# Dilated attention on one core: scores transposed, shifted by a fixed bound instead of row maxima, with the old form behind a flag

## The chip, the cores and the metric

One program runs on one core of one Trainium2 chip (the other seven cores are idle). The metric is the device time of one execution in microseconds (us), of which three runs before the change are known. Beside them stands one profiled execution, from which all durations below are read. The core has a matrix engine (PE, whose weight loads are listed as PEld), a vector engine (DVE), a scalar engine (ACT), a third elementwise engine (POOL) and a queue engine that only issues transfers (SP). Each runs its own list of instructions strictly in the order in which the program holds it, and waits on semaphores where an instruction needs another engine's result.

## The reference

One decoder layer on 2048 positions of 1024 columns: a norm and one input projection; two mixers beside each other, a short gated convolution and an attention of 8 heads of 64 columns; an output projection; a gated feed-forward part. The attention is what the change touches:

```python
q = rms_norm(q.reshape(B, S, N_HEADS, HEAD_DIM), g_q[l]) * (HEAD_DIM ** -0.5)
k = rms_norm(k.reshape(B, S, N_HEADS, HEAD_DIM), g_k[l])
...
for window, dil in ((128, 1), (512, 4), (2048, 16)):     # per head
    # query t attends to keys t, t-dil, ..., t-window
    s = where(valid, q k^T, -inf)
    m = max(s);  e = exp(s - m);  den = sum(e);  o = (e / den) v;  lse = m + log(den)
...
w = softmax(lses over the three branches);  o = sum(w * outs)
```

Since each branch is weighted by its own sum of exponentials, the result is one quotient: the three branches' sums of e·v over the three branches' sums of e, whatever number is subtracted from all scores of a row.

## The kernel before

All products are made in float16 pairs (a high and a low part, three matmuls per product), so a product of two float32 matrices costs three passes of PE.

The program's stages follow one another. First the input norm, the convolution's first three quarters and the weights' preparation. Then attention by four pairs of heads (`attention_pairs`, line 673; g = 0 to 3). Then the output projection (`out_b`) and the feed-forward part (`ffn`), which takes more than half of the span and isn't touched.

Within attention two generators run interleaved. `attn_steps(g)` (line 510) emits the attention of pair g; meanwhile `qkv_steps(g + 1)` (line 444) emits the projection of the next pair: 384 matmuls of 384 columns on PE (lines 188 to 190), then norm, split into high and low halves and three transposing transfers on the SP queue per 512 positions. For g = 3 the rest of the convolution and a first part of the output projection (`tail_steps`) take that place. How many projection steps stand beside one attention step is a number for each g (line 730). The final order on each engine is set by a scheduler ahead of the run.

Per head, `attn_steps` goes through three branches (b = 1, 2, 0: dilation 4, 16, 1), each of 16 tiles of 128 queries against one or two tiles of 128 keys. One step does this for two tiles with two key tiles each (14 steps a head) or for four tiles with one (5 steps a head):

- Scores (lines 612, 613): queries are the stationary operand, keys move, so a PSUM tile `s` has queries on its rows. The moving keys are high and low parts; a query row holds its own high and low part beside each other.
- Mask and row minimum of the negated scores in one DVE instruction per tile (line 618), each followed by a short read of the accumulator.
- Exponential with that row's own shift on ACT, one per tile (line 623).
- Split into float16 high and low: ACT copy (633), DVE subtraction (634).
- The values product needs keys on the rows, so the exponentials are transposed: in the 14 wide steps by a transposing transfer `et<-eh` of 128 x 1024 elements on the SP queue (line 635), in the 5 others by four PE transposes in float32 into PSUM `pt` (line 628).
- Values product (line 641): 128 x 65 columns into `av`, the 65th being the sum; an ACT copy brings it out (line 644).

`combine` (line 542) joins the three branches: their row shifts are compared, weights exp(difference) made, and POOL multiplies and adds 128 x 1040 tiles (lines 556 to 558), then divides (562). For the last head it runs on DVE in four pieces. Branches 1 and 2 go through memory (`d_u`, written in one order of rows and read back as `r` in another).

Queries lie in four-strided order (line 461 takes every fourth position as one tile), so a POOL copy `qn` (line 535) restores plain order for branch 0.

Of the kernel before, what the change touches and what calls it, by code (L numbers as in the profile page):

```python
# [18 lines left out]
P = 128  # L19
# [6 lines left out]
H = 8  # L26
# [4 lines left out]
class Builder:  # L31

# [163 lines left out]
    def run(self):  # L199
        tc, nc, A = self.tc, self.nc, self.A  # L200
        with ExitStack() as ctx:
# [5 lines left out]
            self.d_u = [[dr.tile([S, HD + 2], F32, name=f"d_u{h}_{b}") for b in range(2)] for h in range(H)]  # L207
# [10 lines left out]
            self.eps = cp.tile([P, 3], F32, name="eps")  # L218
            self.wsm = ctx.enter_context(tc.tile_pool(name="wsm", bufs=3))
            self.big = ctx.enter_context(tc.tile_pool(name="big", bufs=1))  # L220
            self.wq = ctx.enter_context(tc.tile_pool(name="wq", bufs=2))
            with ExitStack() as c1:
                e = c1.enter_context
                self.psmm = e(tc.tile_pool(name="psmm", bufs=3, space=PSUM))
                self.qk = e(tc.tile_pool(name="qk", bufs=2))
                self.mixer(c1)

                self.fs = ctx.enter_context(tc.tile_pool(name="fs", bufs=1, side="right"))
                self.fw = ctx.enter_context(tc.tile_pool(name="fw", bufs=15, side="right"))

                self.gs = ctx.enter_context(tc.tile_pool(name="gs", bufs=2, side="right"))
                self.psg = ctx.enter_context(tc.tile_pool(name="psg", bufs=4, space=PSUM, side="right"))
                self.out_b()
            self.ffn()

# [35 lines left out]
    def conv_steps(self, j, W, before=None, scratch=None):  # L271
# [12 lines left out]
        for c in range(S // NC):  # L284
# [49 lines left out]
            if j > 1:  # L334

                ps = self.pstr.tile([P, 4], F32, name="tr") if j < 3 else self.pst.tile([P, 4, P], F32, name="pt")[:, 0, 0:4]
# [107 lines left out]
    def qkv_steps(self, g, st):  # L444
# [8 lines left out]
        qT = self.qk.tile([P, 2, 4, 4, P], F16, name="qT")  # L453
        ka, kl = (self.qk.tile([P, 4, 2, 512], F16, name=nm, bufs=2) for nm in ("ka", "kb"))
        dv = self.d_v[g]
        for i in range(0, NT, 4):
            f = self.at.tile([P, 4, 4, HD], F32, name="qkf", bufs=2)
            for j in range(4):
                vs = self.vs[i // 4 % 2]

                t = slice(j, 4 * P, 4)
# [12 lines left out]
                if j == 3:  # L474
                    nc.sync.dma_start(dv[:, i * P:(i + 4) * P].rearrange("h (p t) c -> p h (t c)", t=4),
                                      vs.rearrange("p h t x d -> p h (t x d)"))
# [26 lines left out]
            for n_, dst in enumerate((qT.rearrange("p h j n t -> p (h j) n t")[:, :, i // 4],  # L503
                                      ka[:, i // 4].rearrange("p h (j t) -> p (h j) t", j=4),
                                      kl[:, i // 4].rearrange("p h (j t) -> p (h j) t", j=4))):
                self.transpose(dst, hl[:, 2 * n_:2 * n_ + 2].rearrange("p h j x d -> p (h j x d)"))
            yield
        st.update(qT=qT, ka=ka, kl=kl)

    def attn_steps(self, g, st):  # L510
# [4 lines left out]
        V, U, R = {}, {}, {}  # L515

        def load_v(h, b):
            dv = self.d_v[g][h]
            t = V[h, b] = self.vp.tile([P, NT, 2 * HD + 2], F16, name="v", bufs=2)
            if b == 1:  # L520
                nc.sync.dma_start(t.rearrange("p (n r) c -> p n (r c)", n=4),
                                  dv.rearrange("(n p r) c -> p n (r c)", n=4, r=4))
            elif b == 2:
                nc.sync.dma_start(t.rearrange("p r c -> p (r c)"), dv.rearrange("(p r) c -> p (r c)", r=16))
            else:

                for r in range(4):
                    nc.sync.dma_start(t[32 * r:32 * r + 32], dv.rearrange("(n p r) c -> r p n c", n=NT, r=4)[r])
        for h, b in [(h, b) for h in range(2) for b in (1, 2, 0)]:
            qT = st["qT"][:, h]  # L530
            ka, kl = (st[x][:, :, h] for x in ("ka", "kl"))
            if b == 1:
                qn = self.at.tile([P, S], F16, name="qn", bufs=1)
                for n in range(4):
                    nc.gpsimd.tensor_copy(qn[:, n * 512:(n + 1) * 512].rearrange("p (t j) -> p t j", j=4),
                                          qT[:, :, n].rearrange("p j t -> p t j"))
            load_v(h, b)


            last = g == 3 and h == 1  # L540

            def combine(c, n):
# [3 lines left out]
                w = self.at.tile([P, 3, NT], F32, name="cw", bufs=2)[:, :, 0:n]  # L546
                X = [r[:, ts] for r in (U[h, 0], R[h, 1], R[h, 2])]
                nc.vector.tensor_tensor(bm, X[0][:, :, HD + 1], X[1][:, :, HD + 1], op=ALU.min)
                nc.vector.tensor_tensor(bm, bm, X[2][:, :, HD + 1], op=ALU.min)
                for q in range(3):  # L550
                    nc.vector.tensor_tensor(w[:, q], bm, X[q][:, :, HD + 1], op=ALU.subtract)
                nc.scalar.activation(w, w, AF.Exp)
                X = [x[:, :, 0:HD + 1] for x in X]
                e = nc.vector if last else nc.gpsimd
                for q in range(3):
                    e.tensor_tensor(X[q], X[q], w[:, q].unsqueeze(2).broadcast_to([P, n, HD + 1]), op=ALU.mult)
                e.tensor_tensor(X[1], X[1], X[2], op=ALU.add)
                e.tensor_tensor(X[0], X[0], X[1], op=ALU.add)
                nc.vector.reciprocal(bm, X[0][:, :, HD])
# [6 lines left out]
            Ub = U[h, b] = self.up.tile([P, NT, HD + 2], F32, name="u", bufs=3)  # L566
            Vb = V[h, b]

            def query(u):

                if b == 0:
                    return qn[:, u * P:(u + 1) * P]
                if b == 1:
                    return qT[:, u % 4, u // 4]
                return qT[:, u % 4].rearrange("p n t -> p (n t)")[:, u // 4::4]

            def keys(tl, u, prev):

                k = tl.rearrange("p n (j t) -> p n j t", j=4)
                n = u // 4  # L580
                if b == 0:
                    m = u % 4
                    k = k.rearrange("p n j (m t) -> p n m j t", m=4)
                    if prev and m == 0:
                        return [k[:, n - 1, 3], k[:, n, 0]]
                    return [k[:, n, m - prev:m + 1]]
                if b == 1:
                    return [k[:, n - prev:n + 1, u % 4]]
                return [k[:, :, u % 4, u // 4::4]]

            mask = self.masks[b == 0]

            def has_prev(u):
                return 1 if (b == 0 and u > 0) or (b == 1 and u >= 4) else 0
            for u0 in (0, 8, 4, 12) if last and b == 0 else range(0, NT, 4):
                av = self.psav.tile([P, 4, HD + 1], F32, name="av")

                four = not has_prev(u0 + 3)
                for us in (range(u0, u0 + 4),) if four else (range(u0, u0 + 2), range(u0 + 2, u0 + 4)):


                    blocks = [(u, x) for u in us for x in range(1 - has_prev(u), 2)]
                    nb = len(blocks)
                    at = {u: slice(P * blocks.index((u, 1 - has_prev(u))), P * blocks.index((u, 1)) + P) for u in us}
                    sp = self.pss.tile([P, 512], F32, name="s")
                    for u in us:
                        pv = has_prev(u)
                        hi, lo = keys(ka, u, pv), keys(kl, u, pv)
                        w = (at[u].stop - at[u].start) // len(hi)
                        for x in range(len(hi)):  # L610
                            o = sp[:, at[u].start + x * w:at[u].start + (x + 1) * w]
# [620 lines left out]
```

## Time and profile before

| | us |
|---|---|
| three runs | 2168.03, 2169.90, 2171.61 (median 2169.90) |
| the profiled execution, whole | 2167.63 |
| its span, first to last instruction | 2165.8 |

| stage in the profiled execution | from, to (us) |
|---|---|
| input norm, convolution, weights, projection of pair 0 | 0 to 295 |
| attention of the four pairs, with the next pair's projection beside it | 295 to 752 |
| last head's end and start of the output projection | 752 to 800 |
| output projection | 800 to 930 |
| feed-forward part | 930 to 2166 |

The stages' limits are read from the first and the last matmul of each kind: the first score matmul starts at 285 us and the last at 751 us, and the last values product at 776 us. PE is busy for 2062.4 us of the span (95%), DVE for 1412.4, ACT for 1031.5 and POOL for 657.8. A matmul's row shows from its issue to its modelled end, so rows of PE overlap and a busy PE can still have room: how closely matmuls start behind one another says more than their duration.

### The profile page before, as it was taken

How to read it: one execution, taken by the hardware profiler on the slowest of the kernel's cores; microseconds unless marked ns; L12 is line 12 of the kernel's file. 1: busy time of each engine (PE TensorE's matmuls, PEld its weight loads, DVE VectorE, ACT ScalarE, POOL GpSimd, SP SyncE). 2: the span in 40 equal slices, each digit the busy share in tenths (PEclk: the TensorE clock that was granted, in tenths of full speed). 3: DMA queues.
4: the chain of work that ended last, by engine and by line, in shares of the span. 5: the costliest groups of instructions: out<-in, count | busy, mean ns of one | idle time of the engine just before them, and what ended most of it. 6: DMA issues, size and time to landing. Idle time of an engine off the chain costs nothing. (4 is left out here: it accounts for less than half of the span.)

```text
span 2165.8 us, 32715 instructions
## 1 busy us (share of the span) xinstructions
PE 2062.4 (95%) x11864; PEld 1071.6 (49%) x11864; DVE 1412.4 (65%) x3206; ACT 1031.5 (48%) x2166; POOL 657.8 (30%) x547
## 2 busy tenths in 40 slices
PE   4899999999898889999999999999999999999999
PEld 2344577777665534444444444444444444444444
DVE  6687437677666866885766666666676665545454
ACT  6443347777765745662433333333333344343341
POOL 0001134454532311310312111211121145555463
PEclk9999999999999989999999999999999999999999
DMA  9867459999989977899332233223322763241442
GB/s 248 170 199 240 125 128 161 209 187 205 192 165 225 207 181 237 231 296 228 102 117 83 93 103 112 88 88 107 112 89 88 253 250 86 88 165 54 128 139 93
DMA packets 555491, 339.63 MB, mean 157 GB/s; under 512 B 354624, under 2 KB 508224, under 8 KB 552896
## 3 DMA queue, kind: packets, MB, share of 16 engines
q1 hardware_dynamic: 537648, 314.38, 56.3%
q10 hardware_dynamic: 17680, 23.16, 3.0%
q8 instruction: 93, 1.52, 0.3%
q14 instruction: 70, 0.57, 0.1%
HBM read 161.24 MB, written 107.54 MB: 124 GB/s over the span
## 5 line engine op out<-in xcount | busy, mean ns | idle before, releaser
L1012 PEld LDWEIGHTS <-w 128*128 128x128 f16 x3696 | 363.0, 98 | 454.4 <-issue 21.7
L1012 PE MATMUL ps<-b,w 128*128 128x512 f16 x2112 | 468.7, 383 | 12.0 <-DMA b<-d_h 4.8
L1143 PE MATMUL ps<-b,w 128*128 128x512 f16 x1848 | 399.8, 379 | 3.8 <-DVE s L1164 2.3
L1012 PE MATMUL ps<-hb,w 128*128 128x512 f16 x1584 | 347.1, 379 | 0.0
L1143 PEld LDWEIGHTS <-w 128*128 128x128 f16 x1848 | 180.8, 98 | 222.6 <-issue 5.2
L905 POOL TENSOR_TENSOR t<-wq 128x512 f32<-128x512 f32 (+1 forms) x46 | 60.0, 1304 | 410.4 <-issue 236.8
L1018 DVE TENSOR_TENSOR s<-ps,s 128x512 f32<-128x512 f32 x220 | 150.0, 683 | 37.0 <-PE ps L1012 36.5
L188 PE MATMUL mm<-wq,b 128*128 128x384 f16 x512 | 167.7, 327 | 0.0
L189 PE MATMUL mm<-wq,b 128*128 128x384 f16 x512 | 167.5, 327 | 0.0
L190 PE MATMUL mm<-wq,b 128*128 128x384 f16 x512 | 167.4, 327 | 0.0
L1150 POOL TENSOR_TENSOR x<-x,s 128x512 f32<-128x512 f32 x72 | 103.6, 1440 | 173.1 <-DVE s L1164 134.1
L1151 DVE SCALAR_TENSOR_TENSOR x<-ps,a_u,x 128x512 f32<-128x512 f32 x96 | 71.8, 749 | 101.4 <-PE ps L1143 74.8
L618 DVE CUSTOM_DVE_ANT_0 s<-s,mask,nkap 128x256 f32<-128x256 f32 (+1 forms) x224 | 104.4, 483 | 41.4 <-PE s L613 37.1
L623 ACT ACTIVATE s<-s,u 128x256 f32<-128x256 f32 (+1 forms) x224 | 100.0, 457 | 37.4 <-DVE u L618 31.6
L922 ACT CAST w<-t 128x512 f16<-128x512 f32 x88 | 53.7, 616 | 132.6 <-PE ps L1012 66.3
L188 PEld LDWEIGHTS <-b 128*128 128x128 f16 x768 | 83.8, 109 | 62.0 <-ACT b L786 8.4
L189 PEld LDWEIGHTS <-b 128*128 128x128 f16 x768 | 83.9, 109 | 56.2 <-issue 6.8
L190 PEld LDWEIGHTS <-b 128*128 128x128 f16 x768 | 83.7, 109 | 54.9 <-issue 2.6
L188 PE MATMUL cvx<-b,wq 128*128 128x512 f16 (+1 forms) x200 | 77.3, 390 | 31.2 <-ACT kb L265 24.9
L641 PE MATMUL av<-v,et 128*128 128x65 f16 x1800 | 77.5, 195 | 29.9 <-DMA et<-eh 22.1
L634 DVE TENSOR_TENSOR eh<-s,eh 128x512 f16<-128x512 f32 (+1 forms) x112 | 75.6, 678 | 35.4 <-ACT eh L633 35.1
L1121 ACT ACTIVATE wq<-wq,asf 128x512 f32<-128x512 f32 x88 | 56.6, 710 | 86.6 <-DMA wq<-d_a 86.6
(302 smaller groups left out, 3783.1 us busy)
## 6 DMA issues: line engine op xcount, KB each, us to landing
d_a<-a ACTq DMA_DIRECT2D x88, 256.0 KB, 2.0
d_wd<-w SPq DMA_DIRECT2D x77, 256.0 KB, 2.0
wq<-d_a SPq DMA_DIRECT2D x64, 256.0 KB, 4.1
b<-d_wd SPq DMA_DIRECT2D x14, 1024.0 KB, 6.4
wraw<-in_w_in_dram SPq DMA_DIRECT2D x24, 512.0 KB, 7.2
d_h<-hl SPq DMA_DIRECT2D x24, 512.0 KB, 3.2
wq<-in_w_gate_dram SPq DMA_DIRECT2D x22, 512.0 KB, 5.2
wq<-in_w_up_dram SPq DMA_DIRECT2D x22, 512.0 KB, 5.4
```

What stands on the lines that cost most here:

```text
L188: self.pe = mm(ps, lhsT=lh(k), rhs=rh(k), start=k == ks[0], stop=False)
L189: mm(ps, lhsT=lh(k), rhs=rl(k), start=False, stop=False)
L190: mm(ps, lhsT=ll(k), rhs=rh(k), start=False, stop=k == ks[-1])
L618: nc.vector.tensor_tensor_reduce(sm[:, at[u]], sp[:, at[u]], mask[:, P - P * has_prev(u):256], accum_out=Ub[:, u, HD + 1:HD + 2], op0=ALU.add,
L623: nc.scalar.activation(sm[:, at[u]], sm[:, at[u]], AF.Exp, scale=-1.0, bias=Ub[:, u, HD + 1:HD + 2])
L634: nc.vector.tensor_tensor(eh[:, w:2 * w], sm[:, 0:w], eh[:, 0:w], op=ALU.subtract)
L641: self.pe_av = nc.tensor.matmul(av[:, u - u0], lhsT=p_, rhs=v_, start=n_ == 0, stop=n_ == len(ops) - 1)
L1012: nc.tensor.matmul(ps[self.BANK[n]], lhsT=w[:, x, k], rhs=b[:, y, k], start=first and k == 0 and q == 0, stop=k == 3 and q == 2, skip_grou ...
L1018: nc.vector.tensor_tensor(t, x, y, op=ALU.add)
L1143: nc.tensor.matmul(ps[self.BANK[n]], lhsT=L[n][:, x, f], rhs=B[n][:, f, y], start=first and f == 0 and q == 0, stop=f == n_f - 1 and q == ...
L1150: nc.gpsimd.tensor_tensor(o, o, s_, op=ALU.add)
L1151: nc.vector.scalar_tensor_tensor(o, bank, u, o, op0=ALU.mult, op1=ALU.add)
```

## The change

The scores are made transposed (keys stationary, queries moving), so that the exponentials come out with keys on the rows, as the values product needs them. No transpose of any kind is left between them. Row maxima can't be had cheaply in this form, so all scores are shifted by one number: both operands are normalised, so no score is above 8 times the largest product of gains (`bound`). The branches then need no weights; `combine` adds three sums and divides.

```diff
-  for u in us:   # each tile of 128 queries: hi, lo = its one or two tiles of keys
-      nc.tensor.matmul(o, lhsT=query(u), rhs=hi[x], start=True, stop=False)
-      nc.tensor.matmul(o, lhsT=query(u), rhs=lo[x], start=False, stop=True)
-      nc.vector.tensor_tensor_reduce(sm[:, at[u]], sp[:, at[u]], mask[...], accum_out=Ub[:, u, HD + 1:HD + 2], ...)
-      nc.scalar.activation(sm[:, at[u]], sm[:, at[u]], AF.Exp, scale=-1.0, bias=Ub[:, u, HD + 1:HD + 2])
-  if four:
-      nc.tensor.transpose(pt[:, x], sm[:, x * P:(x + 1) * P], self.ident32)
...
-  else:
...
-      self.transpose(et, eh)
+  runs = [(u, u, 1) for u in pr]            # b == 2: four tiles
+  runs = [(u, u, 2), (w, w, 1)]             # b < 2: two tiles, and (u - step, u, 1) ahead where there are such keys
+  for kb_, u, n in runs:                    # a tile of keys against n tiles of queries
+      for i, k in enumerate(keys(kb_)):
+          nc.tensor.matmul(sp[:, o:o + n * P], lhsT=k, rhs=queries(u, n), start=i == 0, stop=i == 1)
+  if b < 2:
+      nc.vector.tensor_tensor(sp[:, 0:o], sp[:, 0:o], self.masks[b][:, 512 - o:512], op=ALU.add)
+  nc.scalar.activation(dst, src, AF.Exp, scale=self.kap, bias=self.bound)
+  if b == 2:
+      nc.gpsimd.affine_select(e, e, pattern=[[0, 4], [1, P]], compare_op=ALU.is_ge, fill=0.0, ...)
+  nc.scalar.copy(et[:, 0], e)
+  nc.vector.tensor_tensor(et[:, 1], e, et[:, 0], op=ALU.subtract)
```

A head has 20 steps in place of 19. Positions now stay in plain order: the projection's stationary operand is contiguous (`slice(j * P, (j + 1) * P)`), and the keys of branch 1 and 2 are read as a strided stationary operand, every 4th and every 16th column. The queries of these branches come from a copy `q16` that POOL regroups (32 copies of 512 columns in place of the 32 of `qn`):

```diff
+  o, d = ((u * P, 1), (u // 4 * 512 + u % 4, 4), (u, 16))[b]
+  return [k[:, o:o + (P - 1) * d + 1:d] for k in (ka, kl)]
...
+  self.nc.gpsimd.tensor_copy(st["q16"][h][:, :, 32 * n:32 * n + 32], st["qT"][:, n, h].rearrange("p (a r) -> p r a", r=NT))
...
-  for n_, dst in enumerate((qT..., ka..., kl...)):      # three transposing transfers of 128 x 1024
-      self.transpose(dst, hl[...])
+  self.transpose(qT[:, i // 4]..., hl[:, 0:2]...)       # one of 128 x 1024
+  for h in range(2):
+      for n_, dst in ((2, ka), (4, kl)):                # four of 128 x 512
+          self.transpose(dst[:, h, i * P:(i + 4) * P]..., hl[:, n_ + h]...)
```

`combine` loses its weights and keeps the least sum for a check:

```diff
-  nc.vector.tensor_tensor(bm, X[0][:, :, HD + 1], X[1][:, :, HD + 1], op=ALU.min)
...
-  nc.scalar.activation(w, w, AF.Exp)
-  for q in range(3):
-      e.tensor_tensor(X[q], X[q], w[:, q].unsqueeze(2).broadcast_to([P, n, HD + 1]), op=ALU.mult)
   e.tensor_tensor(X[1], X[1], X[2], op=ALU.add)
   e.tensor_tensor(X[0], X[0], X[1], op=ALU.add)
+  nc.vector.tensor_reduce(self.dmin[:, d:d + 1], X[0][:, :, HD], axis=AX.X, op=ALU.min)
+  nc.vector.tensor_scalar_max(bm, X[0][:, :, HD], 2.0 ** -7)
```

The values `d_v` are written in plain order, two transfers of 130 columns a row in place of one of 520, the rows of `d_u` are 65 columns in place of 66, PSUM has two `av` tiles in place of one and no `pt`, and the steps of projection beside one step of attention are 4.29, 3.32, 3.04 and 2.0 in place of 4.52, 3.49, 3.2 and 2.1.

A fixed shift can make all of a row's exponentials tiny. So the whole old kernel stands behind the new one, as a second program (`General`) that runs if a sum was below 2^-6:

```diff
+  def check(self):
+      nc.vector.tensor_single_scalar(self.dmin, self.dmin, 2.0 ** -6, op=ALU.is_lt)
+      nc.vector.tensor_copy(self.low, self.vmax(self.dmin))
+  def otherwise(self):
+      rv = self.nc.values_load(self.low[0:1].bitcast(I32), min_val=0, max_val=0x3F800000, ...)
+      with self.tc.If(rv > 0):
+          General(self.tc, self.A).run()
```

On the inputs of the reference the least sum, worked out from its own formulas, is 2.9 and the threshold is 0.016, so the flag is 0.

How the order moves. On PE, in the attention of the last pair before the change: `s` are scores, `pt` the float32 transposes, `av` the values product, L188 to L190 the convolution.

```order
L613 LDWEIGHTS qT
L613 MATMUL s<-kb,qT 128x128
L628 MATMUL pt<-ident_99,sm 128x128 x2
L612 LDWEIGHTS qT
L612 MATMUL s<-ka,qT 128x128
L628 MATMUL pt<-ident_99,sm 128x128
L641 LDWEIGHTS et
L641 MATMUL av<-v,et 128x65
```

The same pair after the change, in branch 0: a full step is now six score matmuls, of which four stand here, with the keys `ka`, `kb` as stationary operand.

```order
L627 LDWEIGHTS ka
L627 MATMUL s<-qT,ka 128x256
L627 LDWEIGHTS kb
L627 MATMUL s<-qT,kb 128x256
L627 LDWEIGHTS ka
L627 MATMUL s<-qT,ka 128x128
L627 LDWEIGHTS kb
L627 MATMUL s<-qT,kb 128x128
```

No `pt` row is left, and operands have changed sides. On the SP queue before the change, in the attention of pair 0's second head: `d_u` and `r` are a branch's results on their way through memory, `d_v` and `v` the values, `qkhl` the next pair's queries and keys.

```order
L655 DMA r_4031<-d_u_0_67 128x16x66
L475 DMA d_v_62<-vs_2121 128x2x520
L196 DMA_TRANSPOSE et<-eh 128x6x128
L196 DMA_TRANSPOSE et<-eh 128x8x128 x2
L196 DMA_TRANSPOSE qT<-qkhl 128x8x128
L196 DMA_TRANSPOSE ka<-qkhl 128x8x128
L196 DMA_TRANSPOSE kb<-qkhl 128x8x128
L196 DMA_TRANSPOSE et<-eh 128x8x128
L653 DMA d_u_1_68<-u 128x1056
```

The queue after the change, at the same place:

```order
L667 DMA r_3978<-d_u_0_67 128x16x65
L497 DMA d_v_62<-vs_2132 128x4x130 x2
L198 DMA_TRANSPOSE qT<-qkhl 128x8x128
L198 DMA_TRANSPOSE ka<-qkhl 128x4x128
L198 DMA_TRANSPOSE kb<-qkhl 128x4x128
L198 DMA_TRANSPOSE ka<-qkhl 128x4x128
L198 DMA_TRANSPOSE kb<-qkhl 128x4x128
L665 DMA d_u_1_68<-u 128x1040
```

All `et<-eh` rows are gone, and nothing that PE's values product waits for is queued there but `v`. At the end of the same queue after the change:

```order
L1202 DMA out_dram<-x_15_17552 128x1024
L1202 DMA out_dram<-x_7_17544 128x512
L251 TENSOR_LOAD low
L253 COMPARE_AND_BRANCH
L280 DMA nx_x<-in_x_dram 128x1024 x2
```

Before the change the list ended with the second of these transfers. Now each engine loads the flag and branches over the second program, whose first row is the last one shown.

More of the change, by code (lines that the diff above doesn't have):

```diff
@@ L31 @@
 class Builder:
+    W = HD + 1
     def __init__(self, tc, A):
@@ L206, in run @@
             self.d_v = [dr.tile([2, S, 2 * HD + 2], F16, name=f"d_v{g}") for g in range(4)]
-            self.d_u = [[dr.tile([S, HD + 2], F32, name=f"d_u{h}_{b}") for b in range(2)] for h in range(H)]
+            self.d_u = [[dr.tile([S, self.W], F32, name=f"d_u{h}_{b}") for b in range(2)] for h in range(H)]
             self.d_wq = [dr.tile([P, 2, KC, 384], F16, name=f"d_wq{g}") for g in range(5)]
@@ L218, in run @@
             self.eps = cp.tile([P, 3], F32, name="eps")
+            self.dmin = cp.tile([P, 11], F32, name="dmin")
+            self.low = cp.tile([P, 1], F32, name="low")
             self.wsm = ctx.enter_context(tc.tile_pool(name="wsm", bufs=3))
@@ L452, in qkv_steps @@
         yield
-        qT = self.qk.tile([P, 2, 4, 4, P], F16, name="qT")
-        ka, kl = (self.qk.tile([P, 4, 2, 512], F16, name=nm, bufs=2) for nm in ("ka", "kb"))
+        qT = self.qk.tile([P, 4, 2, 512], F16, name="qT")
+        ka, kl = (self.qk.tile([P, 2, S], F16, name=nm, bufs=2) for nm in ("ka", "kb"))
+        st.update(qT=qT, ka=ka, kl=kl, q16=[self.at.tile([P, NT, P], F16, name="q16", bufs=2), None])
         dv = self.d_v[g]
@@ L577, in keys @@
[L577 to L589, printed above, removed]
@@ new lines, in queries, with keys @@
+                    return q16.rearrange("p (x j) (n a) -> p j n x a", j=4, n=4)[:, u % 4, u // 4:u // 4 + n]
+                return q16[:, u]
+            def keys(u):
+                o, d = ((u * P, 1), (u // 4 * 512 + u % 4, 4), (u, 16))[b]
+                return [k[:, o:o + (P - 1) * d + 1:d] for k in (ka, kl)]
+            step = 4 if b == 1 else 1
+            if b == 1:
+                tiles = [[4 * n + j for j in (j0, j0 + 1) for n in (n0, n0 + 1)] for n0 in (0, 2) for j0 in (0, 2)]
+            else:
+                tiles = [list(range(u0, u0 + 4)) for u0 in ((0, 8, 4, 12) if last and b == 0 else range(0, NT, 4))]
@@ L657, in attn_steps, with pools, few, constants @@
                 combine(0, NT)
+    def pools(self, e):
+        tc = self.tc
+        self.pss = e(tc.tile_pool(name="pss", bufs=3, space=PSUM))
+        self.psav = e(tc.tile_pool(name="psav", bufs=2, space=PSUM))
+    def few(self):
+        return self.pss.tile([P, 512], F32, name="s")[:, 0:4]
+    def constants(self, m, u):
+        nc = self.nc
+        self.masks = []
+        for b in range(2):
+            mask = self.at.tile([P, 512], F32, name=f"mask{b}")
+            nc.gpsimd.memset(mask, 0.0)
+            for x in range(4):
+                sg = 1 if x % 2 else -1
+                t = mask[:, x * P:(x + 1) * P].rearrange("p (x a) -> p x a", x=4)
+                pattern = [[32 * sg, 4], [sg, 32]] if b == 0 else [[sg, 4], [4 * sg, 32]]
+                nc.gpsimd.affine_select(t, t, pattern=pattern, compare_op=ALU.is_ge, fill=-1e30, base=0,
+                                        channel_multiplier=-sg)
+            self.masks.append(mask)
+        self.kap = self.at.tile([P, 1], F32, name="kap")
+        nc.vector.tensor_scalar_mul(self.kap, u, HD ** -0.5 * 2.0 ** -22)
+        self.bound = self.at.tile([P, 1], F32, name="bound")
+        nc.vector.tensor_scalar(self.bound, m, -HD ** 0.5, 15 * math.log(2.0), op0=ALU.mult, op1=ALU.add)
+    RATES = (4.29, 3.32, 3.04, 2.0)
     def attention(self):
```

395 lines of the change are left out of this document (299 added, 96 removed).

## The prediction

> **What bounds the kernel now.** I read the page first, from the top.
>
> ```profile
> span 2165.8 us, 32715 instructions
> ...
> PE   4899999999898889999999999999999999999999
> ...
> PEclk9999999999999989999999999999999999999999
> DMA  9867459999989977899332233223322763241442
> ```
>
> One slice is 54 us. PE is full nearly everywhere; attention (slices 6 to 14) is where it shows gaps, and where the transfer engines are full too. The table of stretches puts numbers on that stage, and beside it the output projection as a dense one.
>
> ```profile
> core 0: us, PE busy (x) PEld busy (x) DVE busy (x) ACT busy (x) POOL busy (x), PEclk, DMA share, GB/s
> 295.00:752.00 457.00, 427.49 (x4242) 318.27 (x4240) 307.90 (x1115) 328.81 (x885) 196.47 (x157) 0.98 0.96 192
> 752.00:800.00 48.00, 37.42 (x197) 16.77 (x198) 33.79 (x124) 20.77 (x52) 7.31 (x12) 0.81 0.83 193
> 800.00:930.00 130.00, 127.11 (x582) 57.18 (x581) 96.90 (x180) 79.17 (x140) 29.60 (x24) 0.99 0.78 232
> ```
>
> In the 457 us of attention PE is busy for 427, and the 16 transfer engines for 96%. DVE (67%), ACT (72%) and POOL (43%) have room. In the 48 us behind it PE loses 10.6 us idle, and its clock is granted at 0.81. Attention is thus bound by PE, with stalls. The table of waits names them, for 295 to 752 us and, in the last row, for 752 to 800:
>
> ```profile
> PEld L641 <- DMA et<-eh: 28.2, 23, 4.5
> PE av L641 <- DMA et<-eh: 20.9, 19, 4.2
> ...
> PE mm L188 <- ACT b L786: 7.8, 2, 6.5
> ```
>
> The first two rows are the same stalls, seen at the weight load and at the matmul: the values product waits for a transposing transfer. I count the larger, 28.2 us, once. How densely PE works between stalls is read from starts in the timeline of PE:
>
> ```profile
> 432.04 0.89 PE L641 MATMUL av<-v,et 128*128 128x65 f16 x24
> 432.77 0.27 PE L612 MATMUL s<-ka,qT 128*128 128x256 f16 x1
> 432.88 0.27 PE L613 MATMUL s<-kb,qT 128*128 128x256 f16 x1
> ...
> 433.76 0.33 PE L188 MATMUL mm<-wq,b 128*128 128x384 f16 x1
> 433.93 0.33 PE L189 MATMUL mm<-wq,b 128*128 128x384 f16 x1
> ...
> 437.89 0.30 PE L612 MATMUL s<-ka,qT 128*128 128x128 f16 x1
> 438.00 0.30 PE L613 MATMUL s<-kb,qT 128*128 128x128 f16 x1
> 438.12 0.30 PE L612 MATMUL s<-ka,qT 128*128 128x128 f16 x1
> ...
> 442.54 0.63 PE L628 MATMUL pt<-ident,sm 128*128 128x128 f32 x4
> 443.01 0.28 PE L613 MATMUL s<-kb,qT 128*128 128x128 f16 x1
> ```
>
> From start to start a score matmul of 256 columns takes 0.11 us, one of the projection (384) 0.17, a values product 0.73/24 = 0.030, and a float32 transpose 0.47/4 = 0.117. The scores of branch 2 (437.89 to 438.12) take 0.117 for 128 columns, twice the 0.055 that half of the 256 row would make: both operands are read there with every fourth element.
>
> **The change part by part.** The sum is made against the profiled execution, 2167.6 us (span 2165.8), which lies 2.3 us under the median of the three runs.
>
> *PE transposes go.* All 160 of them:
>
> ```profile
> L628 PE MATMUL pt<-ident,sm 128*128 128x128 f32 x160 | 28.1, 279 | 0.0
> ```
>
> 160 x 0.117 = 18.7 us of PE's own time on the bounding engine: **-19**.
>
> *Transposing transfers go.* 112 of them, 3.8 us each from issue to landing, and up to four in a row on the queue:
>
> ```profile
> et<-eh SPq DMA_TRANSPOSE x112, 3.8
> ...
> 431.63 3.71 SPq L196 DMA_TRANSPOSE et<-eh  x2
> 436.07 8.40 SPq L196 DMA_TRANSPOSE et<-eh  x4
> ```
>
> The values product then waits for DVE's subtraction directly, so the 28.2 us go: **-28**. The queue keeps `v`, `d_u`, `r`, `d_v` and five transposes per 512 positions where it had three, of the same bytes; with 112 issues fewer ahead of them they come earlier, and of PE's waits in attention none of any size names them now. I cost them at nothing; the cover is that they are prefetched a step or a branch ahead.
>
> *Elementwise work.* For these groups in attention:
>
> ```profile
> L618 DVE CUSTOM_DVE_ANT_0 s<-s,mask,nkap 128x256 f32<-128x256 f32 x215 | 101.5, 488 | 36.6 <-PE s L613 35.1
> L623 ACT ACTIVATE s<-s,u 128x256 f32<-128x256 f32 x214 | 96.4, 461 | 29.7 <-DVE u L618 23.9 <-DVE qkr_t L486 2.5 <-DVE qkr_t L485 0.9
> L634 DVE TENSOR_TENSOR eh<-s,eh 128x512 f16<-128x512 f32 x102 | 69.8, 688 | 32.1 <-ACT eh L633 31.9
> L633 ACT CAST eh<-s 128x512 f16<-128x512 f32 x103 | 61.4, 601 | 15.9 <-DMA et<-eh 14.8
> L623 ACT ACTIVATE sm<-sm,u 128x128 f32<-128x128 f32 x156 | 52.8, 405 | 8.7 <-DVE u L618 8.4
> L618 DVE CUSTOM_DVE_ANT_0 sm<-s,mask,nkap 128x128 f32<-128x128 f32 x156 | 45.4, 346 | 31.9 <-PE pt L628 16.0 <-PE s L613 14.6 <-ACT et L629 1.2
> L618 DVE DVE_READ_ACCUMULATOR2_ANT u<- 128x1 f32 x378 | 44.3, 117 | 0.0
> ...
> L1154 ACT ACTIVATE s<-ps,a_u 128x512 f32<-128x512 f32 x24 | 16.4, 682 | 17.6 <-issue 12.5 <-PE ps L1143 5.1
> ```
>
> DVE loses 101.5 + 45.4 + 44.3 = 191 us and gains 128 masks at about 0.69 (the 634 row), 88: 308 becomes some 205. ACT loses 96 + 53 = 149 and gains 160 exponentials at 0.68 (the 1154 row), 109: 329 becomes some 290. POOL loses the weights of seven heads (21 tiles) and gains 32 selections of 512 columns:
>
> ```profile
> L685 POOL TENSOR_SCALAR_AFFINE_SELECT mask<-mask x4: 292/300/313, 249.4 to 250.2; 128x128 f32<-128x128 f32 x4
> ...
> L556 POOL TENSOR_TENSOR r<-r,cw 128x1040 f32<-128x1040 f32 x14 | 26.7, 1929 | 35.0 <-ACT cw L552 35.0
> ```
>
> 21 x 1.93 = 41 us go, 32 x 4 x 0.30 = 38 come; the copies `q16` take the place of as many `qn`. None of the three becomes the bound of a stage of about 457 - 19 - 28 = 410 us, all of it beside PE. What does lie on a path is new: branch 2 now goes through POOL, and behind a selection wait ACT's copy, DVE's subtraction and PE's values product. POOL is in order, and ahead of a selection can stand a 1.9 us tile or a copy that waits for a transfer. Nothing in the trace prices that wait: at the low end it is nothing (PE has the projection to do), at the high end 32 selections each behind one 1.9 us tile, 61 us. The nearest case is DVE's group of 634, whose waits for ACT cost PE almost nothing; I take **+5**, for eight blocks of four.
>
> *The scores.* Columns are the same; 128 more matmuls are only longer ones cut in two, which costs nothing at 0.055 per 128. What is unknown is a strided stationary operand under short matmuls. If the moving side made the 0.117, branch 2's 256 matmuls fall to 0.055: -16. If the stationary side made it, branch 2 stays, and branch 1's 192 short ones rise by 0.062: +12, its 128 long ones by 0.007: +1. If the wider step of 16 doubles branch 2's, 256 x 0.117 = 30 more: +43. The projection's rows have a stationary operand strided by four before the change and start every 0.17 us for 384 columns, no slower than the 256 rows for their size. So I leave branch 1 as its size makes it and branch 2 at its own old row: **0**, with -16 and +43 as ends.
>
> [...]
>
> *End of attention.* From 752 to 800 us PE loses 10.6 us idle and 0.19 x 37.4 = 7 us of clock, 17.7 in all, part of it to the last transposes and the last head's `combine`, which loses its weights; 7.8 us are a wait for ACT that the change leaves. I take half: **-9** (0 to -18). In attention the clock is 0.98, worth 9 us, a third of which should return with the stalls: **-3** (0 to -9).
>
> *The flag.* Each engine loads a register and jumps. On SP this stands behind the last transfer's issue:
>
> ```profile
> L1179 SPq DMA_DIRECT2D out_dram<-x x17: 332/333/351, 2069.5 to 2162.9; - x17
> ...
> DMA to landing us min/median/max: 2.0/2.6/3.8
> ```
>
> It is hidden if it takes less than the landing (2.0), and costs up to two round trips (7.6) if it isn't: **+2**. If the branch were taken, the whole old program would run behind, some 2166 us; the least sum of 2.9 against 0.016 excludes it.
>
> Sum: -19 - 28 + 5 + 0 - 9 - 3 + 2 = -52, so 2167.6 - 52 = **2116 us**.
>
> **The rivals.**
>
> *Strided keys are slow.* Price +13 to +43, so 2129 to 2159 us. For it: branch 2's row at twice its size. Against it: the projection's strided operand. By the Trainium skill ("SBUF — State Buffer", on its 16-byte lines) reads that touch a line only once pay, which speaks for this rival in branch 2, whose step of 16 float16 is 32 bytes; but by the same rule the old step of 8 bytes should have been free, and the 0.117 differs from that.
>
> *PE fills up.* Moving operands were the slow side (-16), the other half of the end (-9) and the rest of the clock (-6) return, and nothing new waits (-5): 2080 us. For it: the dense stretch 800:930 shows what PE does when fed.
>
> *Slower: the chain between scores and values product.* PE's order is fixed ahead. A step's mask, exponential, copy and subtraction take 0.69 + 0.68 + 0.60 + 0.69 = 2.7 us, and PE's share of a step is about 410/160 = 2.6. If the order leaves only one step between, or ACT's other work (70% busy) holds up the exponential, PE waits in every step. It decides from 0.33 us per step (160 x 0.33 = 52); at 0.5 us the time is 2168 + 28 = 2196 us. For it: PE's waits for the old chain. Against it: that chain was longer by 3.8 us of transfer, and the new order keeps two or three steps between a score and its product in the pieces I read.
>
> **How the numbers follow.** Forecast 0.58 (its own range 2100 to 2132), strided keys 0.18, PE filled 0.15, slower 0.08, anything with the second program 0.01. The range 2085 to 2150 leaves out the slow cases (0.09) and the far halves of the two others. A measurement tells 0.2% (4 us) from no change: faster 0.89, same 0.02, slower 0.09.
>
> **What would show it.** In the profile after: no wait of PE for `et`; about 455 us between the first score and the end that now takes 505; DVE and ACT below 75% there; starts of branch 2's scores 0.055, 0.117 or 0.23 us apart; PE's waits for the subtraction or the selection under 10 us; the span's end 2 to 5 us behind the last store's issue. Wrong would make it: PE waiting in most steps for ACT or DVE, or a jump at the end that takes over 10 us.

## The result and the profile after

| | before, us | after, us |
|---|---|---|
| median | 2168.97 (2167.75 to 2171.61, 4 runs) | 2134.12 (2127.46 to 2136.36, 4 runs) |
| the profiled execution, whole / span | 2167.63 / 2165.8 | 2136.36 / 2134.9 |
| first score matmul | 285.0 | 300.9 |
| last values product | 776.3 | 729.3 |
| first matmul of the feed-forward part | 941.1 | 908.2 |

The ratio is 0.9833 with a 95% interval of 0.9809 to 0.9857: 34.8 us faster by the medians, 31.3 by the two profiled executions. The forecast was 52. The feed-forward part starts 32.9 us earlier, so the whole gain lies ahead of it. I use the stretch from 285 us to the first matmul of the feed-forward part as the stage to compare, since work of the projection and the convolution moves freely within it: the first score starts 15.9 us later because PE takes up the next pair's projection first, and is busy for all of that time. The page of the kernel after, its span and busy tenths:

```profile
span 2134.9 us, 31526 instructions
...
PE   4899999989899899989999999999999999999998
...
PEclk9999999999999899999999999999999999999999
DMA  9866445656575757896233223322332772331442
```

In attention the transfer engines have fallen from mostly 9 tenths to 5 to 7, but PE's row has hardly filled: four 8s there have become three. The table of stretches for this stage, first of the kernel before:

```profile
285.00:941.00 656.00, 613.01 (x5137) 404.31 (x5136) 451.68 (x1444) 439.55 (x1097) 236.33 (x194) 0.97 0.91 200
```

and of the kernel after (columns as in the prediction: length, then PE, PEld, DVE, ACT, POOL busy, PE's clock, DMA share):

```profile
285.00:908.00 623.00, 582.78 (x5108) 360.45 (x5106) 416.21 (x776) 435.42 (x870) 232.47 (x204) 0.97 0.63 163
```

PE is busy 30.2 us less, but idle for 40.2 us where it was 43.0. The change took work off PE and hardly any waiting. The waits of PE's weight loads in the kernel after, from 280 to 800 us, show who took the place of the transfers:

```profile
PEld L649 <- DVE et L644: 27.1, 25, 3.7
PEld L649 <- ACT et L643: 7.9, 14, 1.2
```

29.6 us of waiting for `et<-eh` by the same window (28.2 from 295 to 752 us) have become 27.1 for the subtraction and 7.9 for the copy ahead of it. The groups of instructions show that these cost more than was forecast:

```profile
L644 DVE TENSOR_TENSOR et<-sm,et 128x512 f16<-128x512 f32 (+1 forms) x160 | 148.0, 940 | 70.9 <-ACT et L643 70.0
L638 ACT ACTIVATE sm<-s,bound,kap 128x512 f32<-128x512 f32 (+1 forms) x160 | 146.6, 940 | 45.1 <-DVE s L632 43.0
L643 ACT CAST et<-sm 128x512 f16<-128x512 f32 (+1 forms) x160 | 94.4, 612 | 4.7 <-POOL sm L640 3.0 <-PE av L649 0.8
L632 DVE TENSOR_TENSOR s<-s,mask 128x512 f32<-128x512 f32 (+1 forms) x128 | 80.6, 650 | 26.9 <-PE s L627 26.4
L640 POOL TENSOR_SCALAR_AFFINE_SELECT sm<-sm 128x512 f32<-128x512 f32 x32 | 23.9, 749 | 51.9 <-ACT sm L638 28.5 <-DVE qT L336 19.0 <-DVE et L644 4.3
```

Masks (650 ns) and copies (612) cost what was said. The subtraction takes 940 ns in place of 690 and the exponential 940 in place of 680. The view of the single line shows that the subtraction's mean is not its usual length (minimum, median, maximum):

```profile
L644 DVE TENSOR_TENSOR et<-sm,et x160: 496/693/2757, 304.3 to 728.1; 128x512 f16<-128x512 f32 x120, 128x384 f16<-128x384 f32 x40
```

The median is the forecast's 690, but 39 of 160 take over 1.0 us and 15 over 2.0. The old form's subtraction, with its input in PSUM, never did:

```profile
L634 DVE TENSOR_TENSOR eh<-s,eh x112: 549/687/693, 305.7 to 756.7; 128x512 f16<-128x512 f32 x104, 128x384 f16<-128x384 f32 x8
```

What stands beside the long ones is seen in the timeline, here all engines ahead of PE's longest wait for one:

```profile
679.91 0.56 DVE L644 TENSOR_TENSOR et<-sm,et 128x384 f16<-128x384 f32 x1 [0.54 <-ACT et L643]
...
680.42 2.41 POOL L580 TENSOR_TENSOR r<-r,r 128x1040 f32<-128x1040 f32 x1 [18.59 <-DMA r<-d_u]
680.52 2.85 DVE L335 SCALAR_TENSOR_TENSOR qT<-ka,convw,qT 128x512 f32<-128x512 f32 x1
...
682.91 2.70 POOL L581 TENSOR_TENSOR u<-u,r 128x1040 f32<-128x1040 f32 x1
683.30 2.72 DVE L644 TENSOR_TENSOR et<-sm,et 128x384 f16<-128x384 f32 x1
...
686.08 0.57 PE L649 MATMUL av<-v,et 128*128 128x65 f16 x7 [3.61 <-DVE et L644]
```

Two DVE instructions that take 0.75 and 0.55 us elsewhere each end 0.4 to 0.5 us behind the POOL tile beside them (682.83 and 685.61), and PE waits 3.61 us for the second. Worked out from all 160 subtractions: the 94 with POOL idle beside them take 0.694 us at most, those that start ahead of POOL's instruction keep their usual length (as at 679.91), and each of the 39 over 1.0 us ends a fixed time behind the end of a POOL instruction, 0.41 to 0.42 us at 384 columns and 0.54 to 0.56 at 512, however long it took. That is a hold until POOL's instruction ends and not a sharing of pace. The sum's tiles end only 11 of these 39; the others stand behind the next pair's norm, splits and query copies (lines 510 to 540) and, once, a selection. The masks on the same engine, with one operand in PSUM, do not move (682 to 700 ns at 512 columns).

The Trainium skill ("SBUF — State Buffer", section "SBUF: two separate sides") says that DVE and GpSimd (POOL here) share one port pair of SBUF, that a DVE instruction with two SBUF inputs beside a GpSimd instruction that reads SBUF, or a DVE instruction in a mode that uses both ports, takes it alone, and that whoever comes second waits for the other's whole instruction. The rows agree: 2.85 and 2.72 us beside tiles of 2.41 and 2.70. In the old form the subtraction's input `s` lay in PSUM; after the change it is `sm` in SBUF.

### The profile page after: what moved, and what is told of

Read it like the earlier page. It is cut to its first block, busy times and chain, and to the rows that moved or that the text cites. A ratio compares the mean times of both kernels' runs of the same rounds, so it can differ in the third digit from the quotient of the medians.

```text
span 2134.9 us, 31526 instructions
## 1 busy us (share of the span) xinstructions
PE 2029.4 (95%) x11832; PEld 1021.3 (48%) x11832; DVE 1378.0 (65%) x2538; ACT 1027.4 (48%) x1939; POOL 655.4 (31%) x562
## 5 line engine op out<-in xcount | busy, mean ns | idle before, releaser
L644 DVE TENSOR_TENSOR et<-sm,et 128x512 f16<-128x512 f32 (+1 forms) x160 | 148.0, 940 | 70.9 <-ACT et L643 70.0
L190 PE MATMUL mm<-wq,b 128*128 128x384 f16 x512 | 168.7, 330 | 1.8 <-DVE vs L494 1.8
L638 ACT ACTIVATE sm<-s,bound,kap 128x512 f32<-128x512 f32 (+1 forms) x160 | 146.6, 940 | 45.1 <-DVE s L632 43.0
L649 PE MATMUL av<-v,et 128*128 128x65 f16 x1800 | 90.2, 195 | 28.2 <-DVE et L644 22.3
L190 PE MATMUL cvx<-b,wq 128*128 128x512 f16 (+1 forms) x200 | 77.3, 390 | 31.8 <-DMA b<-ka 24.5
L191 PEld LDWEIGHTS <-b 128*128 128x128 f16 x768 | 75.9, 99 | 63.1 <-issue 9.2
L190 PEld LDWEIGHTS <-b 128*128 128x128 f16 x768 | 75.8, 99 | 62.0 <-ACT b L809 5.0
L192 PEld LDWEIGHTS <-b 128*128 128x128 f16 x768 | 75.7, 99 | 60.9 <-issue 2.7
L649 PEld LDWEIGHTS <-et 128*128 128x128 f16 x1800 | 78.3, 99 | 48.3 <-DVE et L644 27.1
L1067 ACT ACTIVATE sg<-s,w_un 128x512 f32<-128x512 f32 x66 | 47.3, 719 | 106.1 <-DVE s L1041 98.2
```

What stands on the lines that cost most here:

```text
L190: self.pe = mm(ps, lhsT=lh(k), rhs=rh(k), start=k == ks[0], stop=False)
L191: mm(ps, lhsT=lh(k), rhs=rl(k), start=False, stop=False)
L192: mm(ps, lhsT=ll(k), rhs=rh(k), start=False, stop=k == ks[-1])
L638: nc.scalar.activation(dst, src, AF.Exp, scale=self.kap, bias=self.bound)
L644: nc.vector.tensor_tensor(et[:, 1], e, et[:, 0], op=ALU.subtract)
L649: self.pe_av = nc.tensor.matmul(av[:, us.index(u)], lhsT=p_, rhs=v_, start=n_ == 0, stop=n_ == len(ops) - 1)
```

## The experiments

Theory 1: the subtraction is held up by POOL, and PE with it. Theory 2: branch 1's exponential, which writes every fourth element, loads ACT. Theory 3: neither; PE's fixed order puts the values product too close behind its scores, whatever the durations. Theory 4: branch 2's way through POOL. All runs had five rounds beside the kernel before, whose medians lie between 2167.2 and 2168.9 us. "Idle" is the stage's length less PE's busy time in it, from the table of stretches; "waits" are PEld's waits for the subtraction and for the copy. Stage, idle, mean and waits are read from one execution each, whose own time lies up to 6 us from the median.

| run | median, us | ratio (95% interval) | stage | idle | L644 mean, ns | waits |
|---|---|---|---|---|---|---|
| changed, again | 2131.2 | 0.9830 (0.9814 to 0.9846) | 618 | 37.9 | 936 | 24.1 + 9.3 |
| no flag | 2127.3 | 0.9818 (0.9799 to 0.9836) | 616 | 37.5 | 931 | 24.3 + 9.9 |
| sum left out | 2108.0 | 0.9718 (0.9703 to 0.9734) | 594 | 22.8 | 802 | 11.7 + 6.1 |
| plain exponential | 2118.8 | 0.9774 (0.9756 to 0.9791) | 611 | 32.8 | 909 | 21.4 + 4.5 |
| stride on the read | 2120.6 | 0.9787 (0.9774 to 0.9801) | 611 | 31.0 | 895 | 18.0 + 5.0 |
| branch 0 in PSUM | 2123.4 | 0.9799 (0.9782 to 0.9816) | 612 | 33.4 | 877 / 670 | 13.7 + 12.7 |
| branches 0, 1 in PSUM, plain | 2098.4 | 0.9675 (0.9660 to 0.9691) | 586 | 17.8 | 844 / 645 | 6.8 + 5.3 |
| all in PSUM | 2095.1 | 0.9663 (0.9647 to 0.9679) | 585 | 14.1 | 653 | 6.9 + 4.4 |
| sum on DVE | 2126.3 | 0.9805 (0.9788 to 0.9821) | 618 | 37.0 | 789 | 26.3 + 7.2 |
| sum in quarters | 2120.9 | 0.9784 (0.9762 to 0.9805) | 613 | 34.4 | 816 | 23.4 + 7.4 |
| 21 more POOL tiles | 2148.8 | 0.9909 (0.9889 to 0.9930) | 638 | 56.1 | 915 | 37.1 + 9.8 |
| all in PSUM, 21 more tiles | 2109.3 | 0.9725 (0.9705 to 0.9744) | 603 | 26.6 | 652 | 7.5 + 13.2 |

(Two means: subtractions that read SBUF / PSUM.)

**The changed kernel again.** 

> The changed kernel as it is, beside the others on one chip: 2128 to 2136 us; its PE waits for L644 between 22 and 28 us. It says how far one profile of it strays.

Measured 2131.2; the profiled execution is 10 us shorter than the first, its idle time 2.3 us and its waits for the subtraction 3.0 us less, with the same order on every engine. Differences of that size between two profiles say nothing. Differences below are against this run.

**No flag.** Leaves out the jump and the second program.

```diff
-        self.otherwise()
```

> Leaves out the register load and jump at the end and the second program behind it. If the jump is not hidden by the last store: 3 us less (the last matmul to the end of the span 4.1 us as before the change, against 7.2). If it is hidden: no difference, and 7.2 us stay.

DVE's last row and the issue of the last stores, of the changed kernel (span 2134.9):

```profile
2126.80 2.46 SPq L1202 DMA_DIRECT2D out_dram<-x  x2
2128.15 0.75 DVE L1174 SCALAR_TENSOR_TENSOR x<-ps,a_u,x 128x512 f32<-128x512 f32 x1 [1.38 <-PE ps L1166]
```

and DVE's last row without the flag (span 2124.2):

```profile
2120.46 0.75 DVE L1173 SCALAR_TENSOR_TENSOR x<-ps,a_u,x 128x512 f32<-128x512 f32 x1 [1.38 <-PE ps L1165]
```

From DVE's last instruction to the end it is 6.0 us with the flag and 3.0 without: 3.0 us, not hidden. The kernel before has 3.0 too. The medians differ by 3.9, within their intervals.

**The sum left out.** For seven heads POOL neither adds the branches nor divides.

```diff
-  e.tensor_tensor(X[1], X[1], X[2], op=ALU.add)
-  e.tensor_tensor(X[0], X[0], X[1], op=ALU.add)
+  if last: ...                       # the division likewise
```

The number kept for the flag is the greatest sum here and not the least.

> Leaves out the sum over the three branches and its scaling for seven of the eight heads (21 tiles on POOL, 49.5 us in the changed kernel); nothing is put in its place. Theory 1 (the subtraction L644, whose two inputs now both lie in SBUF, is held up while POOL works): the mean of L644 falls from 940 to about 850 ns, PE's waits for it from 27 to about 15 us, time 6 to 12 us less. Theory 2 (the strided exponential loads ACT) and theory 3 (PE's fixed order puts the values product too close behind its scores, whatever the durations): within 3 us.

23 us went, twice the forecast, and idle time fell by 15. POOL's work costs PE time, but this run alone does not say by which way: 29 subtractions still take over 1.0 us, each held by POOL's other work, and the order on PE is a new one.

**A plain exponential in branch 1**, the rows put right by four transfers.

```diff
-  src = src.rearrange("p (n x a) -> p n x a", x=4, a=32)
-  dst = dst.rearrange("p (n a x) -> p n x a", x=4, a=32)
+  dx = du.rearrange("(n a x r) c -> x a n (r c)", n=4, x=4, r=4)
+  for x in range(4):
+      nc.sync.dma_start(dx[x], Ub[32 * x:32 * x + 32].rearrange("p (n r) c -> p n (r c)", n=4))
```

> Branch 1's exponential is written in the order in which it is read; its result goes out through four transfers that put the rows right. Theory 2: the mean of L638 falls from 940 to about 720 ns, ACT does 30 us less in attention, and since DVE and PE wait for ACT in a third of their waits, 5 to 12 us less. Theory 1: L638 falls the same, but PE's waits for the subtraction stay at some 27 us: within 3 us. Theory 3: within 3 us.

L638's mean fell to 765 ns (its line is 634 here), less far than forecast, and 12.4 us went: theory 2, just beyond the upper end. The order on PE differs from the changed kernel's in 150 of 11832 matmuls.

**The stride on the read.** The same permutation, read with gaps and written without.

```diff
-  src = src.rearrange("p (n x a) -> p n x a", x=4, a=32)
-  dst = dst.rearrange("p (n a x) -> p n x a", x=4, a=32)
+  src = src.rearrange("p (n x a) -> p n a x", x=4, a=32)
+  dst = dst.rearrange("p (n a x) -> p n a x", x=4, a=32)
```

> Branch 1's exponential does the same permutation, but reads PSUM in steps of 32 elements and writes SBUF without gaps, where the changed kernel reads without gaps and writes every fourth element. If the write is what takes long (theory 2 as a matter of the destination): 0.78 us for 512 columns in place of 1.29, L638's mean 720 to 770 ns, and the time that of the plain exponential, 2117 to 2123 us. If a permuted pattern takes long on either side: 1.29 us stays and the time is the changed kernel's, 2128 to 2136.

This is the cleanest of the runs, since the order on every engine is the same, row by row, as in the changed kernel. The line's view, of the changed kernel:

```profile
L638 ACT ACTIVATE sm<-s,bound,kap x160: 657/817/1404, 302.1 to 722.0; 128x512 f32<-128x512 f32 x120, 128x384 f32<-128x384 f32 x40
```

and with the stride on the read:

```profile
L638 ACT ACTIVATE sm<-s,bound,kap x160: 653/777/878, 302.0 to 711.2; 128x512 f32<-128x512 f32 x120, 128x384 f32<-128x384 f32 x40
```

The gaps in the written tile were what took 1.3 us for 512 columns. The 64 exponentials of branch 1 took 26.9 us less (146.6 to 119.7 of busy ACT), and the kernel 10.6 us less. With the order unchanged this is duration alone, so theory 3 can't hold for this share. The exponentials without gaps take 0.78 to 0.79 us for 512 columns in both kernels, so 0.68 was too low for them too.

**Exponentials kept in PSUM.** First branch 0 alone:

```diff
-  e = self.ep.tile([P, 512], F32, name="sm", bufs=3)[:, 0:o]
+  e = (sp if b == 0 else self.ep.tile([P, 512], F32, name="sm", bufs=3))[:, 0:o]
```

> Branch 0's exponential is written back to its PSUM tile, so that cast and subtraction read PSUM there. Theory 1: the 64 subtractions of branch 0 take about 0.69 (512 columns) and 0.55 us (384) with hardly any above 1 us, the mean of L644 falls from 940 to about 820 ns, and 4 to 10 us go. Theories 2 and 3: L644 may fall, but the time stays within 3 us. Against both: the tile of scores is held for two operations more, and PE may come to wait for a free one at L627, which would give back up to 5 us.

7.8 us went, as theory 1 had it; the 64 subtractions from PSUM take 0.693 us at most, while 27 of the 96 from SBUF still take over 1.0. Then branches 0 and 1, with the plain exponential:

> Branch 1's exponential written in reading order (as in the run with the plain exponential) and the exponentials of branches 0 and 1 both written back to PSUM; only branch 2 keeps the SBUF tile. If theories 1 and 2 are separate costs, their gains add: 13 us of the plain exponential and 7 to 14 of PSUM, some 2110 us, with L644 at about 0.69 and 0.55 us for the 128 subtractions of these branches and PE's waits for it under 10 us. If theory 3 holds (order, not durations) the second step adds nothing: 2118 us. If the tiles of scores run out, PE's waits at L627 grow past 10 us and it ends above 2118.

and all three, with branch 2's mask added on DVE like the others':

```diff
+  nc.vector.tensor_tensor(sp[:, 0:o], sp[:, 0:o], self.masks[b]..., op=ALU.add)      # b == 2 too
-  nc.gpsimd.affine_select(e, e, pattern=[[0, 4], [1, P]], ...)
```

> As the run before, and branch 2 too: its mask is added on DVE in PSUM like the others' (32 more masks, 32 x 0.69 = 22 us for DVE), the selection on POOL is gone (24 us). Theory 1: all 160 subtractions flat, mean 0.67, 2 to 6 us less than the run before. Theory 4 (branch 2's way through POOL costs PE the +5 of the prediction): also 2 to 6 us less, with the gain at branch 2's values products. Neither: DVE's 22 us stand ahead of subtractions and the time is the same or up to 4 us more.

The subtractions of branches 0 and 1 and, in the same profile, those of branch 2 that still read SBUF:

```profile
L640 DVE TENSOR_TENSOR et<-s,et x128: 542/681/693, 301.4 to 695.8; 128x512 f16<-128x512 f32 x88, 128x384 f16<-128x384 f32 x40
...
L640 DVE TENSOR_TENSOR et<-sm,et x32: 676/693/2411, 332.4 to 677.4; 128x512 f16<-128x512 f32 x32
```

From PSUM the longest takes 0.693 us; from SBUF, beside the same POOL work, 2.411. The second step gives more than the two parts did alone (33 us against 12 and 8, though branch 1's part of PSUM was not run alone). The stage with all in PSUM:

```profile
285.00:870.00 585.00, 570.94 (x5101) 356.21 (x5100) 390.27 (x808) 410.40 (x869) 197.73 (x172) 0.99 0.68 174
```

PE's idle time is 14.1 us where it was 40.2, and its clock 0.99 where it was 0.97. At 2095.1 us this version is faster than both kernels, the changed one by 36 us. Taking branch 2 off POOL, the last step, gave 3.3 us with overlapping intervals. That is net of 32 more masks on DVE and of 32 subtractions that now read PSUM, so theory 4 was not measured by itself; in the changed kernel ACT's copy idled 3.0 us in all for the selection (the row of L643 above). The scheduler wrote a new order for each of the three, so some of these gains may be its; their shares of order and duration were not separated.

**The sum on DVE.**

```diff
-  e = nc.vector if last else nc.gpsimd
+  e = nc.vector
```

> The sum over branches and its scaling of the seven other heads run on DVE, as the last head's do, and not on POOL: 21 tiles, some 1.6 us each there, 34 us more for DVE. Theory 1: what leaving them out gave (some 24 us) comes for the larger part, 10 to 20 us, since a subtraction now stands at most behind 1.6 us and isn't slowed while it runs. If the slowing was not POOL's (a busy DVE delays subtractions as much): within 4 us of the changed kernel, or slower.

A miss for theory 1's forecast: 4.9 us in place of 10 to 20, close to the 4 of the other reading and with overlapping intervals. The subtraction did get shorter (789 ns), but PE waited for it as long as ever (26.3 us). DVE's timeline ahead of PE's longest wait for a values product shows why:

```profile
357.65 1.73 DVE L580 TENSOR_TENSOR r<-r,r 128x1040 f32<-128x1040 f32 x1 [3.00 <-DMA r<-d_u]
359.31 0.68 DVE L644 TENSOR_TENSOR et<-sm,et 128x512 f16<-128x512 f32 x1
```

A subtraction of usual length ends just as late when it stands behind 1.73 us of sum. What counts for PE is when it ends.

**More POOL tiles**, to the changed kernel and to the one with all in PSUM:

```diff
+  [nc.gpsimd.tensor_tensor(X[2], X[2], X[2], op=ALU.add) for _ in range(3)]     # behind each sum
```

> The changed kernel with 21 more POOL tiles, three behind each of the seven sums (a tile that is no longer needed is added to itself; 21 x 2.5 = 52 us, as much as leaving the sum out took away). Theory 1: the mean of L644 rises from 940 to 1050 ns or more, PE's waits for it by 8 us or more, the time 8 to 25 us above the changed kernel's 2131. If POOL's work is only in the way of its own selections and copies, or not at all: L644 stays at 940, and the time within 5 us.

> The same 21 POOL tiles added to the kernel that keeps all exponentials in PSUM (2095 us). Theory 1: its subtractions read one operand from PSUM and stay at 0.65 us in the mean; the time within 5 us. If the tiles cost through anything else (POOL's own order, the copies of queries, the scheduler's new order): it rises like the changed kernel does with them, by 8 us or more.

Theory 1 in this narrow form fell: both kernels lost alike (17.6 and 14.1 us), and L644's mean did not rise. With all in PSUM the subtraction stayed at 652 ns, but others were held. The timeline of DVE, ACT and POOL ahead of a wait of PE of 3.9 us:

```profile
414.54 2.39 POOL L580 TENSOR_TENSOR r<-r,r 128x1040 f32<-128x1040 f32 x1 [5.46 <-DMA r<-d_u]
414.71 2.25 DVE L506 TENSOR_SCALAR qk_ss<-qk_ss 128x16 f32<-128x16 f32 x1 [0.36 <-ACT qkr_t L504]
...
416.88 0.69 DVE L632 TENSOR_TENSOR s<-s,mask 128x512 f32<-128x512 f32 x1
417.01 3.92 POOL L591 TENSOR_TENSOR r<-r 128x1040 f32<-128x1040 f32 x2
417.48 1.48 DVE L507 SCALAR_TENSOR_TENSOR qkr_t<-qkr_y 128x16 f32<-128x16 f32 x1
417.60 0.75 ACT L634 ACTIVATE s<-s,bound,kap 128x512 f32<-128x512 f32 x1 [2.58 <-DVE s L632]
```

Sixteen elements a row in 2.25 us: the next pair's norm (lines 506 to 509, usually 0.17 us) is held beside POOL as the subtraction was, ending 0.03 us behind POOL's tile, and mask, exponential and values product queue behind it. ACT also waits longer for POOL, for its copies at lines 519 and 520 (12.0 us in place of 6.0 with all in PSUM), with exponentials behind. How the 14 us divide between these and the new order stays open.

**The sum in quarters.** The same work on POOL, in 84 instructions in place of 21.

```diff
-  e.tensor_tensor(X[1], X[1], X[2], op=ALU.add)
+  [e.tensor_tensor(X[1][:, j:j + 4], X[1][:, j:j + 4], X[2][:, j:j + 4], op=ALU.add) for j in range(0, n, 4)]
```

> The changed kernel with the 21 POOL tiles of the sum cut into 84 quarters of 260 and 256 columns; the same work, in instructions of about 0.6 us in place of 2.0 to 2.5. If a DVE instruction beside POOL is held until POOL's present instruction ends, shorter ones hold it less: the subtractions over 2.0 us (12 of 160 in the changed kernel) are halved at least, the mean of L644 falls from 940 to about 860 ns, PE's waits for it by 5 us or more, the time 5 to 15 us below 2131. If POOL and DVE share the memory's pace in proportion, whatever an instruction's length: L644's mean and the time (within 4 us) stay.

The changed kernel had 15 subtractions over 2.0 us, not 12; with quarters 3 are left, though POOL was busy for longer (245 us of the stage, not 232). L644's view:

```profile
L644 DVE TENSOR_TENSOR et<-sm,et x160: 541/692/2262, 303.4 to 720.4; 128x512 f16<-128x512 f32 x120, 128x384 f16<-128x384 f32 x40
```

The mean fell to 816 ns and 10.3 us went. The three that are left over 2.0 us stand behind a norm tile (L510) that was not cut. So the length of POOL's single instruction counts, as under a hold until its end, and not only its total work. PE's waits fell less than forecast (24.1 to 23.4), and the order on PE is a new one in 777 of 11832 matmuls: that the subtractions got shorter is shown, that the 10 us come from it is not.

## Why the prediction came out as it did

The time lay inside the whole range, at the upper end of the forecast's own 2100 to 2132 (2134.1, and 2131.2 when run again), and the direction was right. Two thirds of the forecast gain came, with other shares than those of the sum, so part of the hit is luck: a gain on the scores that was put at nothing stood in for waits that did not go. It also falls where the rival of slow strided keys ended (2129 to 2159), whose mechanism did not occur.

- **Transposes, -19: right.** No `pt` row is left.
- **Scores, 0 with an end at -16: the end was nearer.** The moving side had been the slow one. PE's timeline after, in branch 2 at a clock of 1.00:

```profile
441.28 0.22 PE L627 MATMUL s<-q,ka 128*128 128x128 f16 x1
441.34 0.23 PE L627 MATMUL s<-q,kb 128*128 128x128 f16 x1
441.40 0.23 PE L627 MATMUL s<-q,ka 128*128 128x128 f16 x1
441.47 0.22 PE L627 MATMUL s<-q,kb 128*128 128x128 f16 x1
```

  0.06 us from start to start, where it was 0.117. Over all scores that is 11 to 17 us less: 17 with each matmul at its group's median distance (85.5 us before, 68.6 after), 11 with the distances under 0.3 us as they stand (81.3 and 69.9). I had left branch 2 at its own old row although its moving operand became contiguous. The stationary step of 16 elements costs some 0.005 us, so the rival of slow strided keys fell; the rule on 16-byte lines that spoke for it (the Trainium skill, "SBUF — State Buffer", section "Door 1: The DMA port swizzle") doesn't describe these rows.
- **Waits for `et`, -28: the step that failed.** "The values product then waits for DVE's subtraction directly, so the 28.2 us go" took the new chain's length from a row whose input lay in PSUM (line 634) and a row that wrote without gaps and was a scaled copy, not an exponential (line 1154). Both prices were too low: 940 ns each in place of 690 and 680. The waits for the chain are 35.0 us, and the stage's idle time fell by 2.8. It fell by so little although another wait went that the sum did not have: PE's matmuls waited 6.5 us for ACT's copy out of the one `av` tile (line 644) before, and 0.2 with two tiles. The mechanism is the slow rival's, at a lower price: 35.0 us over 160 steps is 0.22 us a step, under the 0.33 from which it would have decided, and it came in 39 waits, not in every step. With prices near the forecast's (653 and 734 ns with all in PSUM) idle time falls by 24 to 26 us more, against the changed kernel's two profiles; that version has a new order, so this says that about as much was to be had, and not which part did it.
- **POOL's selection, +5: not measured by itself.** 3.3 us when taken off POOL, not separated from 0 and net of DVE's new masks; ACT's copy idled 3.0 us for it. That POOL was not the bound was right and beside the point; what it held was DVE.
- **End of attention, -9, and clock, -3: did not come.** PE's wait for ACT's `b` is 4.6 us where it was 7.8, but in the 48 us from 720 on, behind the last scores as 752 to 800 was before, PE is idle for 9.8 us and its clock is 0.82, against 10.6 and 0.81:

```profile
720.00:768.00 48.00, 38.20 (x200) 18.18 (x200) 36.60 (x135) 26.12 (x59) 10.28 (x17) 0.82 0.70 212
```

  The clock of the whole stage is 0.97 as before. Both came with all in PSUM: 4.0 us idle at 0.89 in the same place, and 0.99 in the stage.
- **Flag, +2: 3.0.** The span's end is 5.6 us behind the end of the last store's issue (2129.26), just beyond the 2 to 5 that were said.

- **What was to show it.** 455 us from the first score to the end of that stage were said, where 505 were. Taken to the first matmul into the output projection's own PSUM tile (789.2 before, 752.5 after), 451.5 came, which says less than it seems, since projection work now stands ahead of the first score. DVE (67%) and ACT (70% of the stage) are under 75%, so that no engine became the bound by its sum; PE's waits for the subtraction, said to be under 10 us, are 27.1.

The stage is 33.0 us shorter: 30.2 of PE's busy time, most of it transposes and scores, and 2.8 of idle time. With +3.0 for the flag that is -30.0, against 31.3 less in the profiled execution. The rival in which PE fills up (2080) is what the version with all in PSUM approaches at 2095.

## What to carry to other kernels

A price taken from a row holds only where the operands lie in the same memory with the same steps: with one input moved from PSUM to SBUF, and POOL busy beside it, the subtraction took 0.94 us in the mean in place of 0.69; with gaps in its output the exponential of 512 columns took 1.29 in place of 0.78. On a chain that PE waits for, that gave back a wait as large as the one removed. When a wait is taken away, price its successor with its tail (15 of 160 over 2 us), since PE's fixed order pays for the late ones and not for the mean. An engine that is busy a third of the time can still be in the way through the length of its single instructions; the kernel with them cut up was 10 us faster, and the one that reads from PSUM beside them some 24 (36.1 less the 12.4 of the plain exponential), each with a new order in it.

## What was not expected of the hardware

- A subtraction with both inputs in SBUF, once held, ended 0.41 to 0.42 us (384 columns) or 0.54 to 0.56 us (512) behind the end of a POOL instruction, in all 39 cases of the changed kernel.
- A DVE instruction of 128 x 16 elements with its operands in SBUF took 2.25 us beside a POOL tile of 2.39, 13 times its usual 0.17; masks of 512 columns with one operand in PSUM kept to 682 to 700 ns.
- An exponential of 128 x 512 float32 from PSUM took 1.3 us writing every fourth element and 0.78 reading every 32nd.
- A stationary operand with a step of 16 float16 cost PE 0.005 us per 128 x 128 matmul, a moving one with a step of four 0.06.
